# Side jobs queued behind VectorE's weight splits, in smaller portions, in the pass of u of a hybrid block with product-key experts

## The chip, the cores and the metric

The kernel runs on one core of a Trainium2 chip, as one launch. The metric is the time of one execution in microseconds, here the median of several runs. A core has a matrix engine (TensorE, PE in the profile; its weight loads are PEld), VectorE (DVE), ScalarE (ACT), GpSimd (POOL) and SyncE (SP), which mostly issues DMAs. Each engine works through its own instructions in order.

## The reference

One layer over 512 tokens of 1024 features, in float32: a norm, a mixer of differential attention and a gated linear recurrence, an output projection, and then a layer of 16384 experts that are picked per token. The last part is what the change touches, and it is this:

```python
q = (xt @ w_q).reshape(T, 8, 2, 128)
s = einsum('thcd,hcnd->thcn', q, sub_keys)          # 128 keys a side
s1, i1 = top_k(s[:, :, 0], 16)
s2, i2 = top_k(s[:, :, 1], 16)
cand = s1[..., :, None] + s2[..., None, :]          # 256 sums per head
cand_idx = i1[..., :, None] * 128 + i2[..., None, :]
top_s, top_pos = top_k(cand, 16)
expert_idx = take_along_axis(cand_idx, top_pos)
gate = softmax(top_s)
# per token: 8 heads x 16 experts = 128 of 16384
hidden = einsum('td,tkd->tk', xb, u[idx])
act = gelu(hidden) * g
out = einsum('tk,tkd->td', act, v[idx])
```

## The kernel before

The 512 tokens are four blocks of 128. For the last three blocks (384 tokens) the expert layer is computed densely: all 16384 rows of u are multiplied with the tokens in a first pass, the result goes through Gelu, is multiplied with a matrix G that holds each token's gates at its 128 experts and zero elsewhere, and a second pass multiplies with all rows of v. The first block is computed as the reference writes it, with gathers of 128 rows of u per step.

The pass of u is the loop `for c in range(P)` at L718, one chunk of 128 experts each. `dense_u(c)` (L525) loads 512 KB of u (`wu`, a DMA that SyncE issues), splits them into a rounded high part `hi` (ScalarE, L160) and the remainder `lo` (L164), and runs 24 matmuls: 8 pieces of the feature axis, each with hi x hi, hi x lo and lo x hi (L534). The remainder is VectorE's for every third chunk (c = 0, 3, 6, ...) and GpSimd's for the two others (`U_SPLIT`). There are four buffers each of `wu`, `hi` and `lo`, and two PSUM banks of H. ScalarE empties a bank by a Gelu (`gl`, L539) and stores the result to memory (`a_d`); the last 43 chunks stay on chip.

Beside this, the loop hands out two generators' work before each chunk. `jobs` is the chain of routing block 1, building its G, and the same for blocks 2 and 3. `route(b)` is the two levels of top-16 on VectorE (L347 to L351; `sc`, `v`, `i` are the 128-key level and `cand`, `tv`, `ti` the level of 50 candidates a head), the one-hot look-up of indices (`oh` L389 and `ef` L391 on VectorE, `ov` L390 on GpSimd), and the gates: a subtraction on VectorE (L394), `Exp` on ScalarE (L395), sum and division. `build_gates(b)` turns the indices into numbers (`f`, L417), transposes them on TensorE (`tpg`, L420 and L421), compares them with a ramp (`A` L444, `B` L448), scales by the gates (`Bg` L451), multiplies on TensorE (`gq` L456), and stores G (`g_d`). `ug` is `gather_u(0)`: GpSimd issues a gather of 128 rows (`gt`, L469, three buffers), and VectorE forms the dot with the tokens (L472) one step later. After the last dot ScalarE takes one Gelu of them (`hid`, L474).

Each `yield` names a weight; `more(gen, budget)` (L703) steps a generator until the weights reach the budget, `JOBS` = 2.6 and `DOTS` = 2.4 a chunk. What a step takes beyond the budget is not counted later. This sets the order in which the program is traced. A scheduler then lists the instructions of each engine by a simulated time; what is traced under `tc.high_priority()`, as the split is, goes ahead of the rest that is ready.

Block 0's routing runs before the loop, on the same names; its last parts overlap the loop's first chunks.

Of the kernel before, what the change touches and what calls it, by code (L numbers as in the profile page):

```python
# [3 lines left out]

# [7 lines left out]
F32 = mybir.dt.float32  # L12
# [10 lines left out]
P = 128  # L23
# [13 lines left out]
TD = ND * P  # L37
TB = 32
GG = 4
JOBS = 2.6  # L40
DOTS = 2.4
U_SPLIT = ('av', 'ap', 'ap')
V_SPLIT = ("av", "av", "av")
GS = 4096.0
# [9 lines left out]
def block_kernel(ctx: ExitStack, tc: tile.TileContext, a: dict, out: bass.AP):  # L54
# [89 lines left out]
    def mix_t(o, mixedT, i, gain):  # L144
# [6 lines left out]
        nc.scalar.activation(hi, tp, AF.Copy, scale=gain)  # L151
        nc.vector.scalar_tensor_tensor(lo, tp, gain, hi.bitcast(F32), op0=ALU.mult, op1=ALU.subtract)

    def split(src, how="av"):

        hi = wts.tile([P, D], F32R, name="hi", tag="hi", bufs=WS)
        lo = wts.tile([P, D], F32R, name="lo", tag="lo", bufs=WS)
        s = src.rearrange("p k c -> p (k c)") if len(src.shape) == 3 else src
        if how[0] == "a":
            nc.scalar.activation(hi, s, AF.Copy)  # L160
        else:
            nc.vector.tensor_copy(hi, s)
        eng = nc.gpsimd if how[1] == "p" else nc.vector
        eng.tensor_tensor(out=lo, in0=s, in1=hi.bitcast(F32), op=ALU.subtract)  # L164
        return hi, lo

    last = [None]
# [187 lines left out]
    def route(b):  # L355
        v16 = mid.tile([P, 16, 16], F32, name="v16", tag="v16", bufs=EARLY)
        i16 = mid.tile([P, 16, 16], U32, name="i16", tag="i16", bufs=EARLY)
        for r in range(16):
            if r % 2 == 0:
                sc = mid.tile([P, 2, P], F32, name=f"sc{b}", tag="sc", bufs=3)  # L360
                nc.sync.dma_start(sc, sc_d[b, r // 2])
            top16(v16[:, r, :], i16[:, r, :], sc[:, r % 2, :], P)
            yield 1.0
        i16f = mid.tile([P, 8, 2, 16], F32, name="i16f", tag="i16f", bufs=1)
        nc.vector.tensor_copy(i16f.rearrange("p h c k -> p (h c) k"), i16)
        vv = v16.rearrange("p (h c) k -> p h c k", c=2)
        nc.vector.tensor_scalar_mul(i16f[:, :, 0, :], i16f[:, :, 0, :], float(P))
        cand = mid.tile([P, 8, NCAND], F32, name="cand", tag="cand", bufs=1)
        cidx = mid.tile([P, 8, NCAND], F32, name="cidx", tag="cidx", bufs=1)
        for dst, s1, s2 in ((cand, vv[:, :, 0, :], vv[:, :, 1, :]), (cidx, i16f[:, :, 0, :], i16f[:, :, 1, :])):  # L370
            o = 0
            for i, w in enumerate(CAND_W):
                nc.vector.tensor_tensor(out=dst[:, :, o:o + w], in0=s2[:, :, 0:w], in1=s1[:, :, i:i + 1].to_broadcast([P, 8, w]),  # L373
                                        op=ALU.add)
                o += w
            nc.vector.tensor_tensor(out=dst[:, :, o:o + 8], in0=s1[:, :, 8:16], in1=s2[:, :, 0:1].to_broadcast([P, 8, 8]),
                                    op=ALU.add)
        tv = mid.tile([P, 8, 16], F32, name="tv", tag="tv", bufs=1)
        ti = mid.tile([P, 8, 16], U32, name="ti", tag="ti", bufs=1)
        for r in range(8):  # L380
            top16(tv[:, r, :], ti[:, r, :], cand[:, r, :], NCAND)
            yield 0.7
        tif = mid.tile([P, 8, 16], BF16, name="tif", tag="tif", bufs=1)
        nc.vector.tensor_copy(tif, ti)
        ef = mid.tile([P, 8, 16], F32, name="ef", tag="ef", bufs=1)
        for r in range(8):
            oh = mid.tile([P, NCAND, 16], BF16, name="oh", tag="oh", bufs=1)
            ov = mid.tile([P, 16, NCAND], F32, name="ov", tag="ov", bufs=1)
            nc.vector.tensor_tensor(out=oh, in0=iota_c, in1=tif[:, r, None, :].to_broadcast([P, NCAND, 16]), op=ALU.is_equal)  # L389
            nc.gpsimd.tensor_tensor(out=ov.rearrange("p k c -> p c k"), in0=oh, in1=cidx[:, r, :, None].to_broadcast([P, NCAND, 16]), op=ALU.mult)  # L390
            nc.vector.tensor_reduce(ef[:, r, :], ov, axis=AX.X, op=ALU.add)  # L391
            yield 1.4
        g = mid.tile([P, 8, 16], F32, name=f"gate{b}", tag="gate" if b else "gate0")
        nc.vector.tensor_tensor(out=g, in0=tv, in1=tv[:, :, 0:1].to_broadcast([P, 8, 16]), op=ALU.subtract)  # L394
        nc.scalar.activation(g, g, AF.Exp)  # L395
        gs = mid.tile([P, 8], F32, name="gs", tag="gs", bufs=1)
        nc.vector.tensor_reduce(gs, g, axis=AX.X, op=ALU.add)
        nc.vector.reciprocal(gs, gs)
        nc.vector.tensor_tensor(out=g, in0=g, in1=gs[:, :, None].to_broadcast([P, 8, 16]), op=ALU.mult)
        gates[b] = g  # L400
        if b:
            sel[b] = (ef, g)
            return
        ei = mid.tile([P, P], I32, name="ei")
        nc.vector.tensor_copy(ei, ef.rearrange("p h k -> p (h k)"))
        eidx[b] = ei

    def build_gates(b):
# [7 lines left out]
        nc.vector.tensor_single_scalar(i12[:, 1, :], ei, P - 1, op=ALU.bitwise_and)  # L416
        nc.vector.tensor_copy(f12, i12)  # L417
        tp = psu.tile([P, 4, P], F32, name="tpg", tag="tp")
        for i in range(2):
            nc.tensor.transpose(tp[:, i, :], f12[:, i, :], ident)  # L420
        nc.tensor.transpose(tp[:, 2, :], g.rearrange("p h k -> p (h k)"), ident)  # L421
        sT = bld.tile([P, 2, P], F16, name=f"sT{b}", tag="sT", bufs=1)
        nc.vector.tensor_copy(sT, tp[:, 0:2, :])
        gT = bld.tile([P, P], F32, name=f"gT{b}", tag="gT", bufs=1)
# [100 lines left out]
    def dense_u(c):  # L525
        w = wts.tile([P, KC, P], F32, name="wu", tag="w")
        u_load[0] = nc.sync.dma_start(w, a["uT"][c])
        with tc.high_priority():
            hi, lo = split(w, U_SPLIT[c % 3])
        H_ps = psu.tile([P, 512], F32, name="H", tag="H", bufs=2)[:, :TD]  # L530
        for k in range(KC):
            ks = slice(k * P, (k + 1) * P)
            for i, (x, y) in enumerate(((hi, X[0]), (hi, X[1]), (lo, X[0]))):
                nc.tensor.matmul(H_ps, x[:, ks], y[:, k, P:], start=k + i == 0, stop=k == KC - 1 and i == 2)  # L534
        if c >= P - sum(KEEP):
            gl = kept_gl[c] = next(slots)
        else:
            gl = den.tile([P, TD], F32, name="gl", tag="gl", bufs=3)
        nc.scalar.activation(gl, H_ps, AF.Gelu)  # L539
        if c not in kept_gl:  # L540
            nc.scalar.dma_start(a_d[c], gl)

# [157 lines left out]
    vgen = gather_v(0)  # L700
    vp = None

    def more(gen, budget):  # L703
        while budget > 0:
            x = next(gen, None)
            if x is None:
                return False
            budget -= x
        return True

    for c in range(P):
        if vp is None and not more(jobs, JOBS):
            bldx.close()
            vp = ctx.enter_context(tc.tile_pool(name="vp", bufs=2, side="right", reuse_waits="tile"))
            load_g(order[0])
            kept[False] = ctx.enter_context(tc.tile_pool(name="keep2", bufs=1, side="right", reuse_waits="tile"))
        if not more(ug, DOTS) and c < V0_UNTIL:
            next(vgen, None)  # L718
        dense_u(c)
    assert vp is not None  # L720
    psu_x.close()
# [97 lines left out]
```

## Time and profile before

| | us |
|---|---|
| median of 3 runs | 1653.03 (1651.81 to 1653.68) |
| the profiled execution | 1650.1 |
| its span | 1648.3 |
| TensorE busy | 1565.3 (95%) |
| VectorE busy | 1164.1 (71%) |
| ScalarE busy | 633.7 (38%) |
| GpSimd busy | 732.3 (44%) |

The span runs from the first instruction to the last. The profiled execution's own time is 1.8 us longer than its span and 2.9 us under the median. The pass of u starts at 431.32 us and the pass of v at 1102.76; what lies before is the mixer and the scores of the routing. Busy time is an average over stages with different limits, so it is read by stretch. A wait is put down to the instruction that came last.

### The profile page before, as it was taken

The page shows a single profiled execution, that of the slowest core. Times are in us where ns is not written, and L with a number is a line of the kernel's source. Part 1 is how long each engine was busy: PE and PEld are TensorE (multiplying, and loading weights), DVE is VectorE, ACT ScalarE, POOL GpSimd, SP SyncE. Part 2 cuts the span into 40 slices and gives each one's busy share as a digit, 9 for nine tenths or more (in the row PEclk, how much of TensorE's full clock was granted, in tenths as well). Part 3 has the DMA queues.
Part 4 walks back from the last instruction along what each step waited for, and adds up shares of the span by engine and source line. Part 5 has one row for each costly group of instructions (what it writes and reads, how often), then busy time and mean ns, then how long its engine had stood idle before and what let it go on. Part 6 is the DMA issues. An engine that isn't in the chain of part 4 may idle for free.

```text
span 1648.3 us, 22390 instructions
## 1 busy us (share of the span) xinstructions
PE 1565.3 (95%) x8045; PEld 1367.9 (83%) x8045; DVE 1164.1 (71%) x2268; ACT 633.7 (38%) x979; POOL 732.3 (44%) x457
## 2 busy tenths in 40 slices
PE   7999987799989889998999999999999999999998
PEld 5788755588989889898999999998888888888886
DVE  5065553535799899987677665458988888888874
ACT  4475444323333233433443443333333333333332
POOL 3533311433356977775655566643332323323300
PEclk9999988899999989998999999999999999999999
DMA  4421201434546867787888879899999999999982
GB/s 170 156 94 65 77 26 61 156 127 160 172 160 205 300 221 273 250 324 280 292 291 317 286 290 319 300 321 338 381 351 330 335 333 325 340 348 322 342 281 103
DMA packets 173900, 404.70 MB, mean 246 GB/s; under 512 B 14523, under 2 KB 95675, under 8 KB 172252
## 3 DMA queue, kind: packets, MB, share of 16 engines
q1 hardware_dynamic: 124684, 252.31, 44.3%
q0 software_dynamic: 36864, 134.23, 23.0%
q10 hardware_dynamic: 12240, 16.72, 2.8%
q8 instruction: 63, 1.03, 0.2%
q14 instruction: 49, 0.40, 0.1%
HBM read 351.63 MB, written 51.58 MB: 245 GB/s over the span
## 4 chain that ended last, share of the span: by engine, by line
PE 55%; DVE 15%; DMA 2%; POOL 1%; issue 1%; ACT 0%; POOLq 0%; DVEq 0%; ACTq 0%
PE y L576 32%; PE H L534 19%; PE gq L456 4%; DVE gt L472 2%; DVE lo L164 2%; DVE Bg L451 1%; DMA gt<-in_u,ei 1%; DVE ef L391 1%; DVE oh L389 1%; DVE B L448 1%; DVE A L444 1%; DVE cand L373 1%; POOL ov L390 0%; POOL lo L164 0%; DVE sc L349 0%
## 5 line engine op out<-in xcount | busy, mean ns | idle before, releaser
L534 PE MATMUL H<-Xh,hi 128*128 128x384 f32 x1024 | 348.8, 341 | 9.2 <-ACT gl L539 7.9
L534 PE MATMUL H<-Xh,lo 128*128 128x384 f32 x1024 | 348.6, 340 | 3.2 <-DVE lo L164 2.2
L534 PE MATMUL H<-Xl,hi 128*128 128x384 f32 x1024 | 349.5, 341 | 0.0
L482 POOL DMA_INDIRECT gv<-in_v,ei x128 | 154.1, 1204 | 336.2 <-DVE tail L486 303.6
L160 ACT ACTIVATE hi<-wu 128x1024 fp32r<-128x1024 f32 x128 | 135.8, 1061 | 329.2 <-PE H L534 243.8
L164 POOL TENSOR_TENSOR lo<-wu,hi 128x1024 fp32r<-128x1024 f32 x85 | 213.2, 2508 | 105.5 <-ACT hi L160 104.7
L576 PE MATMUL y<-lo,ah 128*128 128x512 f32 x768 | 241.8, 395 | 0.0
L576 PE MATMUL y<-hi,ah 128*128 128x512 f32 x768 | 241.8, 396 | 0.0
L576 PE MATMUL y<-hi,al 128*128 128x512 f32 x768 | 241.8, 395 | 0.0
L534 PEld LDWEIGHTS H<-Xh,hi 128*128 128x128 f32 x1024 | 195.2, 191 | 10.8 <-ACT gl L539 9.2
L469 POOL DMA_INDIRECT gt<-in_u,ei x128 | 158.3, 1237 | 102.4 <-DVE hid L472 71.2
L534 PEld LDWEIGHTS H<-Xh,lo 128*128 128x128 f32 x1024 | 195.2, 191 | 4.5 <-DVE lo L164 3.0
L534 PEld LDWEIGHTS H<-Xl,hi 128*128 128x128 f32 x1024 | 195.5, 191 | 0.0
L567 ACT ACTIVATE ah<-act 128x384 fp32r<-128x384 f32 x128 | 67.1, 525 | 332.0 <-issue 278.1
L472 DVE CUSTOM_DVE_ANT_0 gt<-gt,hn2p 128x1024 f32<-128x1024 f32 x128 | 153.3, 1212 | 52.7 <-DMA gt<-in_u,ei 52.6
L576 PEld LDWEIGHTS y<-hi,ah 128*128 128x128 f32 x768 | 144.4, 188 | 34.9 <-ACT gkFalse L539 0.2
L576 PEld LDWEIGHTS y<-hi,al 128*128 128x128 f32 x768 | 144.4, 188 | 34.8
L576 PEld LDWEIGHTS y<-lo,ah 128*128 128x128 f32 x768 | 144.4, 188 | 34.7
L486 DVE SCALAR_TENSOR_TENSOR tail<-gv,hid,tail 128x1024 f32<-128x1024 f32 x127 | 162.7, 1281 | 11.0 <-DMA gv<-in_v,ei 10.3
L164 DVE TENSOR_TENSOR lo<-wv,hi 128x1024 fp32r<-128x1024 f32 x128 | 156.2, 1220 | 10.3 <-ACT hi L160 10.1
L160 ACT ACTIVATE hi<-wv 128x1024 fp32r<-128x1024 f32 x128 | 134.4, 1050 | 13.9 <-DMA wv<-in_v 7.3
L568 DVE TENSOR_TENSOR al<-act,ah 128x384 fp32r<-128x384 f32 x128 | 73.7, 576 | 72.6 <-ACT ah L567 69.4
(258 smaller groups left out, 2389.6 us busy)
## 6 DMA issues: line engine op xcount, KB each, us to landing
wu<-in_uT SPq DMA_DIRECT2D x128, 512.0 KB
wv<-in_v SPq DMA_DIRECT2D x128, 512.0 KB
g_d<-gs SPq DMA_DIRECT2D x12, 2048.0 KB
G<-g_d SPq DMA_DIRECT2D x32, 768.0 KB
a_d<-gl ACTq DMA_DIRECT2D x85, 192.0 KB
gr<-a_d SPq DMA_DIRECT2D x85, 192.0 KB
w_in<-in_w_in SPq DMA_DIRECT2D x28, 512.0 KB
w_q<-in_w_q SPq DMA_DIRECT2D x16, 512.0 KB
```

The source lines that it names most:

```text
L160: nc.scalar.activation(hi, s, AF.Copy)
L164: eng.tensor_tensor(out=lo, in0=s, in1=hi.bitcast(F32), op=ALU.subtract)
L373: nc.vector.tensor_tensor(out=dst[:, :, o:o + w], in0=s2[:, :, 0:w], in1=s1[:, :, i:i + 1].to_broadcast([P, 8, w]), op=ALU.add)
L456: nc.tensor.matmul(gq[:, t, :], A[:, (t4 + t) // 2, :, t % 2], Bg[:, i, t4 // 4, :, t], start=i == 0, stop=i == 1)
L469: nc.gpsimd.indirect_dma_start(out=t, out_offset=None, in_=a["u"], in_offset=bass.IndirectOffsetOnAxis(ap=ei[:, k:k + 1], axis=0))
L472: nc.vector.tensor_tensor_reduce(out=t, in0=t, in1=hn2p, scale=1.0, scalar=0.0, op0=ALU.mult, op1=ALU.add, accum_out=hid[:, k:k + 1])
L482: nc.gpsimd.indirect_dma_start(out=t, out_offset=None, in_=a["v"], in_offset=bass.IndirectOffsetOnAxis(ap=eidx[b][:, k:k + 1], axis=0))
L486: nc.vector.scalar_tensor_tensor(acc, t, w, acc, op0=ALU.mult, op1=ALU.add)
L534: nc.tensor.matmul(H_ps, x[:, ks], y[:, k, P:], start=k + i == 0, stop=k == KC - 1 and i == 2)
L567: nc.scalar.activation(ah, act, AF.Copy)
L568: nc.vector.tensor_sub(al, act, ah.bitcast(F32))
L576: nc.tensor.matmul(y[b][j], x[:, cs], z[:, j * 512:(j + 1) * 512], start=c == order[0] and i == 0, stop=c == order[-1] and i == 2)
```

## The change

`split` notes VectorE's latest split of a chunk in a table `at`, and `dense_u` notes TensorE's last H matmul and ScalarE's Gelu. `behind(engine)` opens `tc.issue_after(at[engine])`: what is traced in it is ordered behind the noted instruction where it runs on the same engine, and no data passes between them. All steps of `jobs` and `ug` are traced behind VectorE's latest split, the Exp of routing behind ScalarE's latest Gelu, and the transposes behind TensorE's latest H. Both get a `yield 1.5` ahead of them. The table is emptied before the loop. The budgets become 1.7 and 1.25, and what a step takes beyond its budget is taken off the next chunk's. A branch that `V0_UNTIL` = 0 had switched off is gone.

```diff
-JOBS = 2.6
-DOTS = 2.4
+JOBS = 1.7
+DOTS = 1.25
...
+    at = {}
+
+    def behind(engine):
+        return tc.issue_after(at[engine]) if engine in at else nullcontext()
...
-        eng.tensor_tensor(out=lo, in0=s, in1=hi.bitcast(F32), op=ALU.subtract)
+        i = eng.tensor_tensor(out=lo, in0=s, in1=hi.bitcast(F32), op=ALU.subtract)
+        if how[1] != "p":
+            at["DVE"] = i.ins
...
-        nc.scalar.activation(g, g, AF.Exp)
+        yield 1.5
+        with behind("ACT"):
+            nc.scalar.activation(g, g, AF.Exp)
...
-        for i in range(2):
-            nc.tensor.transpose(tp[:, i, :], f12[:, i, :], ident)
-        nc.tensor.transpose(tp[:, 2, :], g.rearrange("p h k -> p (h k)"), ident)
+        yield 1.5
+        with behind("PE"):
+            for i in range(2):
+                nc.tensor.transpose(tp[:, i, :], f12[:, i, :], ident)
+            nc.tensor.transpose(tp[:, 2, :], g.rearrange("p h k -> p (h k)"), ident)
...
-                nc.tensor.matmul(H_ps, x[:, ks], y[:, k, P:], start=k + i == 0, stop=k == KC - 1 and i == 2)
+                mm = nc.tensor.matmul(H_ps, x[:, ks], y[:, k, P:], start=k + i == 0, stop=k == KC - 1 and i == 2)
+        at["PE"] = mm.ins
...
-        nc.scalar.activation(gl, H_ps, AF.Gelu)
+        at["ACT"] = nc.scalar.activation(gl, H_ps, AF.Gelu).ins
...
+    credit = {}
+
     def more(gen, budget):
-        while budget > 0:
+
+        left = credit.get(gen, 0.0) + budget
+        while left > 0:
             x = next(gen, None)
             if x is None:
                 return False
-            budget -= x
+            left -= x
+        credit[gen] = left
         return True
 
+    at.clear()
     for c in range(P):
-        if vp is None and not more(jobs, JOBS):
+        with behind("DVE"):
+            busy = more(jobs, JOBS)
+        if vp is None and not busy:
...
-        if not more(ug, DOTS) and c < V0_UNTIL:
-            next(vgen, None)
+        with behind("DVE"):
+            more(ug, DOTS)
         dense_u(c)
```

The lines that the profile calls L394, L395, L417, L420 and L451 are L402, L405, L427, L432 and L463 in the changed file. In the lists below the names are those of the section on the kernel; a number behind a name tells apart tiles of one name.

VectorE ahead of the first block's gate subtraction (`gate_3543`, for which ScalarE's first Exp waits), from behind the split of chunk 6, before:

```order
L349 MATCH_REPLACE cand<-tv,cand 128x50 x8
L348 MAX_INDEX i_5931<-v_5930,sc_5932 128x8 x2
L348 MAX_INDEX i_5931<-v_5930,sc_5944 128x8 x2
L347 MAX v_5930<-sc_5996 128x8
L365 CAST i16f<-i_2582 128x256
L350 MAX tv<-cand 128x8 x8
L349 MATCH_REPLACE sc_5932<-v_5930,sc_5932 128x128 x2
L349 MATCH_REPLACE sc_5944<-v_5930,sc_5944 128x128 x2
L348 MAX_INDEX i_5931<-v_5930,sc_5996 128x8
L367 TENSOR_SCALAR i16f<-i16f 128x8x16
L351 MAX_INDEX ti<-tv,cand 128x8 x8
L394 TENSOR_TENSOR gate_3543<-tv 128x128
```

and now:

```order
L357 MATCH_REPLACE cand<-tv,cand 128x50 x8
L373 CAST i16f<-i_2582 128x256
L358 MAX tv<-cand 128x8 x8
L375 TENSOR_SCALAR i16f<-i16f 128x8x16
L359 MAX_INDEX ti<-tv,cand 128x8 x8
L402 TENSOR_TENSOR gate_3543<-tv 128x128
```

The searches, the replacements and the maximum of the 128-key level (the rows with `sc_`), which belong to a later block, no longer stand there; the six rows of block 0 are the same.

VectorE around the conversion of block 1's indices (`f`, which TensorE's first transposes read; `sT` is the transposes' result on its way back), before; the split shown is chunk 33's:

```order
L472 ISA gt,hid_3619<-gt,hn2p 128x1024
L472 ISA hid_3619 128x1
L415 TENSOR_SCALAR i_3930<-ej_3929 128x128
L416 TENSOR_SCALAR i_3930<-ej_3929 128x128
L367 TENSOR_SCALAR i16f<-i16f 128x8x16
L417 CAST f_3931<-i_3930 128x256
L472 ISA gt,hid_3619<-gt,hn2p 128x1024
L472 ISA hid_3619 128x1
L391 TENSOR_REDUCE ef<-ov 128x16
L389 TENSOR_TENSOR oh<-iota_c,tif 128x800
L164 TENSOR_TENSOR lo<-wu,hi 128x1024
L423 CAST sT_3940<-tpg 128x256
```

and now; the split at the end is chunk 30's:

```order
L484 ISA gt,hid_3614<-gt,hn2p 128x1024
L484 ISA hid_3614 128x1
L427 CAST f_4064<-i_4063 128x256
L484 ISA gt,hid_3614<-gt,hn2p 128x1024
L484 ISA hid_3614 128x1
L484 ISA gt,hid_3614<-gt,hn2p 128x1024
L484 ISA hid_3614 128x1
L435 CAST sT_4110<-tpg 128x256
L437 TENSOR_SCALAR gT_4112<-tpg 128x128
L456 TENSOR_TENSOR A<-iota_n,sT_4110 128x2048
L460 TENSOR_TENSOR B<-iota_n,sT_4110 128x2048
L170 TENSOR_TENSOR lo<-wu,hi 128x1024
```

Before, the conversion stands behind chunk 30's split, with chunk 33's split five rows after it and the copy `sT` behind that; now it stands behind chunk 27's split (not shown), and the copy and the first A and B stand ahead of chunk 30's. A dot and its second row (`hid`, which reads out the sum) stand between. `oh` and `ef` of the next block are no longer among these rows.

## Rows read from the trace of the kernel before

**Rows 1.** The page: the kernel's span.
```profile
span 1648.3 us, 22390 instructions
```

**Rows 2.** By stretch: us, engines' busy us, TensorE's clock, DMA share, GB/s.
```profile
431.00:751.00 320.00, 285.40 (x1680) 277.53 (x1679) 306.11 (x810) 116.29 (x164) 219.84 (x118) 0.95 0.70 241
751.00:1102.00 351.00, 349.69 (x2173) 344.16 (x2173) 219.55 (x260) 136.72 (x206) 210.36 (x128) 1.00 0.86 303
```

**Rows 3.** The chain by time: start us, us, what.
```profile
770.08 1.88 PE gq L456 x16
771.95 13.52 PE H L534 x78
1102.76 534.61 PE y L576 x2291
```

**Rows 4.** Timeline of TensorE, first H: start us, us, operation.
```profile
431.32 0.42 PE L534 MATMUL H<-Xh,hi 128*128 128x384 f32 x1
```

**Rows 5.** Waits of TensorE, 431 to 751 us: total us, times, longest.
```profile
PE tpg L420 <- DVE f L417: 15.1, 2, 7.7
PE gq L456 <- DVE Bg L451: 8.4, 5, 2.5
PE H L534 <- ACT gl L539: 7.9, 3, 6.9
PE H L534 <- DVE lo L164: 2.2, 1, 2.2
```

**Rows 6.** By stretch, after two long waits of TensorE.
```profile
468.00:475.00 7.00, 7.00 (x32) 7.00 (x33) 7.00 (x30) 2.73 (x4) 5.16 (x3) 0.78 0.55 183
751.00:765.00 14.00, 14.00 (x91) 13.37 (x91) 10.94 (x13) 6.07 (x10) 10.22 (x6) 0.88 0.70 225
```

**Rows 7.** Timeline, splits of u's chunks on VectorE (DVE) and GpSimd (POOL).
```profile
432.77 1.20 DVE L164 TENSOR_TENSOR lo<-wu,hi 128x1024 fp32r<-128x1024 f32 x1
619.61 3.57 DVE L164 TENSOR_TENSOR lo<-wu,hi 128x1024 fp32r<-128x1024 f32 x1
619.67 2.41 POOL L164 TENSOR_TENSOR lo<-wu,hi 128x1024 fp32r<-128x1024 f32 x1
748.99 1.21 DVE L164 TENSOR_TENSOR lo<-wu,hi 128x1024 fp32r<-128x1024 f32 x1
```

**Rows 8.** The chain by time, two stretches.
```profile
459.38 1.05 DVE i L348 x4
463.15 1.45 DVE ti L351 x8
...
727.17 14.62 DMA gt<-in_u,ei
```

**Rows 9.** VectorE, 431 to 751: xcount, busy us, mean ns, idle before.
```profile
L472 DVE CUSTOM_DVE_ANT_0 gt<-gt,hn2p 128x1024 f32<-128x1024 f32 x46 | 55.1, 1207 | 11.3 <-DMA gt<-in_u,ei 11.3
L164 DVE TENSOR_TENSOR lo<-wu,hi 128x1024 fp32r<-128x1024 f32 x20 | 33.6, 1682 | 0.0
L391 DVE TENSOR_REDUCE ef<-ov 128x16 f32<-128x800 f32 x32 | 31.1, 973 | 1.6 <-POOL ov L390 1.6
L389 DVE TENSOR_TENSOR oh<-iota_c,tif 128x800 bf16<-128x800 bf16 x32 | 28.5, 890 | 0.0
L451 DVE TENSOR_TENSOR Bg<-B,gp 128x2048 f16<-128x2048 f16 x20 | 27.2, 1390 | 0.0
L444 DVE TENSOR_TENSOR A<-iota_n,sT 128x2048 f16<-128x2048 f16 x10 | 17.8, 1778 | 0.0
```

**Rows 10.** Timeline of ScalarE around the first Exp.
```profile
454.11 1.28 ACT L395 ACT_TABLE_LOAD   x1 [0.39 <-ACT gl L539]
464.82 0.31 ACT L395 ACTIVATE gate<-gate 128x128 f32<-128x128 f32 x1 [9.43 <-DVE gate L394]
467.38 0.49 ACT L539 ACTIVATE gl<-H 128x384 f32<-128x384 f32 x1
```

**Rows 11.** Groups on VectorE, 751 to 1102: the dots.
```profile
L472 DVE CUSTOM_DVE_ANT_0 gt<-gt,hn2p 128x1024 f32<-128x1024 f32 x83 | 99.4, 1215 | 41.4 <-DMA gt<-in_u,ei 41.3
```

More of the change, by code (lines that the diff above doesn't have):

```diff
@@ L1 @@
 import math
-from contextlib import ExitStack
+from contextlib import ExitStack, nullcontext
 from functools import partial
```

## The prediction

> **What bounds the kernel now.** I read the page's span first, then the windows by stage, then what TensorE waits for, then the chain, then VectorE's groups. The span is 1648.3 us [rows 1]. In the stage in which u is multiplied (431 to 1102.76 us, where the chain takes up the y matmuls and stays with TensorE for the last 534.61 us [rows 3]) two halves differ: until 751 us TensorE is busy 285.40 of 320 us and VectorE 306.11, that is 96%; after it TensorE is busy 349.69 of 351 and VectorE 219.55 [rows 2]. So VectorE paces the first half and TensorE the second. The v pass is TensorE's own and nothing of the change reaches it.
>
> TensorE's own work in the pass: the chain has 78 H matmuls in 13.52 us, 0.1733 each, so 4.16 us for a chunk's 24, and 1.88 us for 16 gq [rows 3]. 128 chunks make 532.4, the 48 gq blocks 90.0, the transposes some 1.6: 624 us. The pass lasts from the first H at 431.32 [rows 4] to 1102.76, 671.4, so 47 us are lost. By cause, in the first half [rows 5]: transposes tpg behind the conversion f 15.1 (2 times), gq behind Bg 8.4 (5 times), H behind the Gelu that empties its bank 7.9 (one wait is 6.9), H behind VectorE's split 2.2: 33.6 in all. The rest is small gaps and half clock: in the 7 us after the long wait before 468 TensorE was busy throughout at a granted 0.78, and in the 14 us after the wait before 751 at 0.88 [rows 6]; the levels are 1.2 and 2.4 GHz, so these cost 7 x 0.22 = 1.5 and 14 x 0.12 = 1.7 us.
>
> The same from VectorE's side: its split for chunk 3 starts at 432.77, the one for chunk 60 at 748.99 [rows 7]: 316.2 us for 57 chunks. TensorE needs for 57 chunks with the 20 gq blocks of that stretch 57 x 4.16 + 20 x 1.88 = 274.7, so about 41.5 of the 47 us arise here.
>
> **The change part by part.**
>
> *Less VectorE work before chunk 60.* Smaller amounts (1.7 and 1.25 for 2.6 and 2.4), with the overshoot now charged to the next chunk, spread the jobs over more chunks. Counted over VectorE's new order from the split of chunk 3 to that of chunk 60, against the old: 149 fewer small routing instructions (409 to 260), 8 fewer oh and ef (32 to 24), 6 more dots (45 to 51), 2 more A and B each, 4 more Bg. Small ones: four index searches took 1.05 and eight of the 50-wide kind 1.45 [rows 8], so 0.18 to 0.26 each: 27 to 39, taken at 33. ef and oh are 0.97 and 0.89: 14.9 less. Dots 1.21, A 1.78 (B taken alike), Bg 1.39 [rows 9]: 7.3 + 7.1 + 5.6 = 20 more. Net 28 us less (22 to 34). VectorE's stretch shrinks from 316 to about 288, its gather waits of 11.3 [rows 9] included. TensorE now needs 57 x 4.16 + 24 x 1.88 = 282 there. The two engines come out nearly even: VectorE stops being the pace by a hair, not by a margin.
>
> *What was taken out of there* (the third block's top-16, two dozen Bg, the rest of the dots) lands behind chunk 60, where VectorE has 351 - 220 = 131 us free [rows 2]. I cost it at nothing. If that cover fails, every VectorE microsecond beyond it would show on TensorE at full price; the count for chunks 60 to 126 goes from some 212 to 250 us against 66 x 4.16 + 24 x 1.88 = 320, so it does not.
>
> *Transposes.* In the old order the first conversion f stands behind the split of chunk 30, yet TensorE takes its transposes at chunk 30.2, a stretch in which VectorE was far behind; now f stands behind the split of chunk 27 and TensorE takes them at chunk 26.8. f comes three dots, an ef and the splits' own 1.2 later, some 6 us or 1.4 chunks; VectorE's rows from chunk 3 to 30 add up to 109 us against 27 x 4.16 + 8 (the Exp's stall) = 120 on TensorE, so it is the full lead of its four buffers ahead by then and both long waits (7.7 and 7.4) [rows 5] go. What is late next is gq: the first Bg now ends VectorE's stretch after chunk 30, the first gq waits at chunk 30.2. A Bg with its inputs is up to four instructions behind: 1.4 (one Bg) to 5.6 (four). I take 2.5, the longest Bg wait of before. The second transposes 1 (0 to 2), later gq 3 (0 to 5, for five waits of 8.4 before).
>
> *First Exp.* It waits on ScalarE from 455.4 to 464.82 for VectorE's first subtraction, with a Gelu queued behind it until 467.38 [rows 10]; TensorE stalls 6.9 us there. Routing 0 is not put behind anything, and in the new order the Exp stands behind four Gelus instead of five: one chunk, 4.16, sooner. Before the subtraction stand ten 128-wide searches, maxima and replacements fewer, and some 3 more of them ahead of the split: 13 x 0.26 = 3.4 sooner at most, 2.6 at least. The wait becomes 6.9 + 4.16 - 3.0 = 8.1 (7.7 to 8.5): this stall stays, slightly dearer. Exps 2 to 4 move to 10, 43 and 84 Gelus deep and cost nothing on TensorE as long as VectorE is there in time.
>
> *Edges.* issue_after adds only an order on one engine; no instruction is added. The added waits are instructions queued behind jobs on VectorE: while a job's dot waits for its gather, the next split waits too, and TensorE behind it once its four buffers are through.
>
> *DMAs.* SP's loads of the third routing's scores now stand between the wu of chunks 70 and 76, and one waits for VectorE's top-16 of the buffer: 0 to 3, taken 1.5. g_d stores and the first G load keep several chunks of margin: 0. The wait near 1094 for the last dot stays: 1.5.
>
> *Half clock.* One long stall remains for three: 4 (2 to 6), from the 1.5 and 1.7 above and a little for each short one.
>
> Sum of losses after: 8.1 + 2.5 + 1 + 3 + 1.5 + 1.5 + 4 + 2 (small gaps) = 23.6 against 47: 23.5 us less. Span 1624.8, and with the 1.8 us around the span, 1626.6 for an execution like the profiled one at 1650.1. The median of before was 1653.0, 2.9 above it, so I predict 1630 us. With the small gaps at 1 to 3, the low ends add up to 13.6 of loss (1620), the high ends to 34.6 (1641).
>
> **A rule weighed.** A split on VectorE that ran beside GpSimd's split (3.57 from 619.61; GpSimd's 2.41 from 619.67) took three times the 1.20 of an undisturbed one [rows 7]; over 20 splits the mean was 1.682 [rows 9], an excess of 0.48 x 20 = 9.6 us. The Trainium skill, "SBUF — State Buffer" (The single rule), says that a VectorE instruction with two SBUF inputs and a GpSimd instruction that reads SBUF exclude each other for the whole instruction. The pair at 619.6 agrees. By the rule at its full, taken as the worst case, two GpSimd splits of 2.4 in each of the 19 stretches from chunk 3 to 60 would hold VectorE 91 us, the even balance above would be lost, and the sum would come out above 1700. By the rows the splits lose a tenth of that, the same pairs stood side by side before, and the measured durations of the other groups hold their share already: 1630. I go by the rows and give the rule no chance beyond its part in (a).
>
> **The rivals.**
>
> (a) *VectorE still paces chunks 30 to 54.* The balance is 282 to 288, so 6 us of excess, and another 6 to 10 of gather or GpSimd blocking, pass on to TensorE. For it: VectorE at 96% [rows 2] and a gather seen 14.62 us under way [rows 8]. Against it: four buffers of lead. Losses 23.6 + 12 to 16, 36 to 40: median about 1643 (1641 to 1649).
>
> (b) *Nearly every wait goes.* VectorE keeps ahead from chunk 20 and only the Exp and the end remain: loss about 13, median about 1619. Against it: the even balance.
>
> (c) *It does not do what it says.* The waits move: Exp plus 1.2, transposes replaced by gq waits of the same size, loss 44 to 50: median 1650 to 1656.
>
> (d) *Slower: dots in front of the splits.* Every dot now stands in VectorE's queue between splits, spread evenly, and waits there for its landing. Place: chunks 18 to 60. The wait per dot is 11.3 / 46 = 0.25 us before 751 and 41.4 / 83 = 0.50 after [rows 9, 11]. At 0.50 the 51 dots add 12.7 us (that is case a); it decides from 0.25 + 23.5 / 51 = 0.71 us per dot. At 1.0, where gathers run beside 512 KB loads and the a_d stores, 38 us more: median about 1668; at 0.9, 1663. Against it: three gather buffers are issued ahead, and a slower VectorE gives them time.
>
> **How the numbers follow.** Forecast 0.52, (a) 0.18, (b) 0.08, (c) 0.07, (d) 0.15. A measurement of this kernel tells about 0.2%, 3.3 us, from no change. Faster: 0.52 + 0.18 + 0.08 = 0.78; the same: 0.07; slower: 0.15. The forecast's own range is 1620 to 1642 with what runs differ by. The range that holds 8 of 10 takes in (a) and half of (c) above, and the most of (b) below: 1617 to 1654.
>
> **What would show it.** Right: in the profile after, TensorE's wait for f is gone or under 2 us, its wait at the first Gelu after the Exp is 7.5 to 8.5 at about 463 us, the y matmuls begin near 1079, VectorE's splits are 12.5 to 17 us apart through chunk 60, and the first half's VectorE share falls under 93%. Wrong: H waiting on VectorE's split in several places (a, d), Bg waits above 8 us together (c), gather waits on VectorE of more than 36 us before chunk 60 (d), or a pass that still lasts over 665 us.

## The result

The changed kernel takes 1631.31 us (median of 4 runs, 1629.26 to 1632.68) against 1652.42 for the kernel before: a ratio of 0.9873, 95% interval 0.9856 to 0.9891. Run again beside three experiments it was 0.9911 (0.9879 to 0.9943) of before. The prediction was 1630 us, 1626.6 for the profiled execution; that one took 1629.26, with a span of 1627.5.

The chain and TensorE's timeline of the changed kernel (start us, us, what) bound the pass of u, beside [rows 3, 4]:

```profile
431.44 0.42 PE L546 MATMUL H<-Xh,hi 128*128 128x384 f32 x1
...
1081.91 534.62 PE y L589 x2291
```

It runs from 431.44 to 1081.91: 650.5 us against 671.4. The v pass behind it lasts 534.62, before 534.61. With the same 624 us of own work TensorE loses 26.5 us and not 47.4. The busy time by stretch in the changed kernel, beside [rows 2], and then in three shorter stretches (columns as there):

```profile
431.00:751.00 320.00, 303.24 (x1854) 296.72 (x1853) 283.81 (x606) 125.79 (x180) 218.91 (x121) 0.98 0.76 268
751.00:1082.00 331.00, 327.52 (x2006) 322.98 (x2005) 247.36 (x465) 128.35 (x190) 213.60 (x125) 0.99 0.84 296
431.00:560.00 129.00, 115.03 (x651) 113.25 (x649) 112.41 (x335) 46.31 (x61) 89.86 (x50) 0.97 0.65 219
560.00:640.00 80.00, 77.21 (x484) 75.12 (x485) 78.44 (x167) 29.48 (x44) 57.67 (x33) 0.97 0.85 296
640.00:760.00 120.00, 120.00 (x778) 117.19 (x777) 101.96 (x134) 52.88 (x79) 77.00 (x44) 1.00 0.84 311
```

and the three of the kernel before:

```profile
431.00:560.00 129.00, 119.19 (x676) 117.59 (x675) 122.10 (x534) 47.64 (x63) 79.33 (x43) 0.97 0.60 202
560.00:640.00 80.00, 65.72 (x372) 63.48 (x372) 77.20 (x156) 26.36 (x37) 63.53 (x37) 0.89 0.74 247
640.00:760.00 120.00, 109.49 (x694) 104.99 (x693) 114.12 (x131) 46.63 (x71) 83.21 (x44) 0.94 0.78 281
```

Up to 560 us TensorE is busy less than before (115.03 for 119.19). From 560 to 640 it gains 11.5 us and from 640 to 760 another 10.5, with the clock at 1.00 in the last: the gain lies between about chunk 27 and chunk 60, and VectorE has 12 us less to do from 640 to 760. At the end of that stretch it is VectorE that waits. Between 706 and 748 us it stands idle for ScalarE's `hi` and for TensorE's gq; before the change it had neither wait ahead of 751 (VectorE's waits, 431 to 751):

```profile
DVE lo L170 <- ACT hi L166: 8.6, 3, 4.5
DVE A L456 <- PE gq L468: 7.9, 3, 3.9
```

What TensorE still waits for in the whole pass (total us, times, longest), beside [rows 5]:

```profile
PE tpg L432 <- DVE f L427: 9.3, 2, 7.1
PE H L546 <- ACT gl L552: 6.2, 1, 6.2
PE H L546 <- POOL lo L170: 2.8, 3, 1.3
PE gq L468 <- DVE Bg L463: 1.9, 2, 1.3
```

These are 20.2 us; the rest of the 26.5, some 6, is half clock and small gaps. One of the two long transposes' waits is still there, now at 562 us. The wait behind the first Exp is 6.2 us, a little shorter than before, on ScalarE:

```profile
459.77 0.31 ACT L405 ACTIVATE gate<-gate 128x128 f32<-128x128 f32 x1 [8.47 <-DVE gate L402]
462.34 0.49 ACT L552 ACTIVATE gl<-H 128x384 f32<-128x384 f32 x1
```

The Exp comes 5.05 us sooner than in [rows 10].

How far TensorE has come, read from the timeline: the start of each chunk's first H behind that of chunk 0, in us, and at last the first y matmul. The kernels are those of the next section.

| kernel | chunk 18 | 30 | 48 | 60 | first y |
|---|---|---|---|---|---|
| before | 84.2 | 138.8 | 255.3 | 332.4 | 671.3 |
| changed | 83.0 | 145.7 | 247.6 | 314.8 | 650.3 |
| changed, again | 83.7 | 146.4 | 248.2 | 319.9 | 655.4 |
| amounts alone | 84.2 | 139.2 | 255.8 | 329.7 | 674.3 |
| orderings alone | 85.3 | 150.8 | 260.6 | 329.3 | 668.6 |
| without VectorE's ordering | 84.2 | 138.6 | 252.7 | 324.7 | 660.5 |
| VectorE's ordering alone | 85.2 | 146.6 | 247.9 | 319.1 | 654.3 |
| late Exp | 82.4 | 143.6 | 246.1 | 321.7 | 657.2 |
| splits to VectorE | 83.7 | 143.2 | 261.6 | 328.5 | 660.6 |
| dots from 36 | 84.2 | 149.8 | 260.0 | 326.8 | 687.0 |
| late Exp and dots from 36 | 82.9 | 146.5 | 244.5 | 312.7 | 673.4 |
| dots' amount 2.4 | 83.7 | 146.3 | 256.2 | 334.2 | 671.0 |
| transposes held | 83.8 | 138.5 | 247.8 | 316.2 | 675.9 |
| transposes held, late Exp | 80.9 | 136.0 | 245.1 | 314.7 | 671.2 |

Each row is one execution. Two executions of the changed kernel differ by 0.7 us at chunks 30 and 48 and by 5.1 at chunk 60 and at the first y.

A chunk's place does not tell all of TensorE's work, since gq blocks stand between the chunks, and not the same number in each kernel: ahead of chunk 48 there are 10 before and 14 now. With TensorE's own work taken off (4.16 us a chunk and 1.88 a gq block, as in the prediction), this is what it has lost by the start of a chunk, in us:

| kernel | chunk 30 | 48 | 60 |
|---|---|---|---|
| before | 14.0 | 36.8 | 47.1 |
| changed | 20.9 | 21.6 | 21.9 |
| changed, again | 21.6 | 22.2 | 27.0 |
| orderings alone | 25.7 | 34.6 | 34.6 |
| late Exp | 18.8 | 20.1 | 28.9 |
| splits to VectorE | 16.5 | 31.8 | 31.9 |
| dots from 36 | 17.5 | 28.3 | 28.3 |
| late Exp and dots from 36 | 14.2 | 14.5 | 16.1 |
| dots' amount 2.4 | 21.5 | 30.2 | 41.4 |
| transposes held | 13.7 | 23.6 | 32.7 |
| transposes held, late Exp | 11.2 | 21.0 | 34.8 |

### The profile page after: what moved, and what is told of

The parts are those of the page before. It is cut to its first block, busy times and chain, and to the rows that moved or that the text cites. A ratio compares the mean times of both kernels' runs of the same rounds, so it can differ in the third digit from the quotient of the medians.

```text
span 1627.5 us, 22379 instructions
## 1 busy us (share of the span) xinstructions
PE 1560.2 (96%) x8045; PEld 1363.0 (84%) x8045; DVE 1169.7 (72%) x2268; ACT 634.1 (39%) x979; POOL 733.9 (45%) x457
## 4 chain that ended last, share of the span: by engine, by line
PE 82%; DVE 9%; DMA 3%; POOL 3%; issue 2%; ACT 1%; SPq 0%; POOLq 0%; DVEq 0%; ACTq 0%
PE y L589 33%; PE H L546 22%; PE acct L212 7%; PE acc L197 5%; PE gq L468 5%; PE accq L197 5%; POOL ov L398 1%; DVE gt L484 1%; DMA gt<-in_u,ei 1%; PE sp L349 1%; POOL lo L170 1%; DVE oh L397 1%; PE hsc L266 1%; PE lg L311 1%; DMA wu<-in_uT 1%
## 5 line engine op out<-in xcount | busy, mean ns | idle before, releaser
L481 POOL DMA_INDIRECT gt<-in_u,ei x128 | 164.8, 1288 | 82.1 <-DVE hid L484 48.5
L484 DVE CUSTOM_DVE_ANT_0 gt<-gt,hn2p 128x1024 f32<-128x1024 f32 x128 | 153.6, 1210 | 47.6 <-DMA gt<-in_u,ei 47.4
L589 PEld LDWEIGHTS y<-hi,ah 128*128 128x128 f32 x768 | 143.6, 187 | 35.6 <-ACT gkFalse L552 0.2
L589 PEld LDWEIGHTS y<-lo,ah 128*128 128x128 f32 x768 | 143.6, 187 | 35.6
L589 PEld LDWEIGHTS y<-hi,al 128*128 128x128 f32 x768 | 143.6, 187 | 35.6
L170 DVE TENSOR_TENSOR lo<-wv,hi 128x1024 fp32r<-128x1024 f32 x128 | 156.0, 1219 | 18.8 <-ACT hi L166 18.2
L166 ACT ACTIVATE hi<-wv 128x1024 fp32r<-128x1024 f32 x128 | 134.3, 1049 | 12.5 <-issue 5.5
```

The source lines that it names most:

```text
L170: i = eng.tensor_tensor(out=lo, in0=s, in1=hi.bitcast(F32), op=ALU.subtract)
L481: nc.gpsimd.indirect_dma_start(out=t, out_offset=None, in_=a["u"], in_offset=bass.IndirectOffsetOnAxis(ap=ei[:, k:k + 1], axis=0))
L484: nc.vector.tensor_tensor_reduce(out=t, in0=t, in1=hn2p, scale=1.0, scalar=0.0, op0=ALU.mult, op1=ALU.add, accum_out=hid[:, k:k + 1])
L589: nc.tensor.matmul(y[b][j], x[:, cs], z[:, j * 512:(j + 1) * 512], start=c == order[0] and i == 0, stop=c == order[-1] and i == 2)
```

## The experiments

All are edits of the changed kernel. Ratios are to the kernel before on the same chip. The changed kernel itself ran beside the last three edits alone; the others are compared with it by their ratios.

**Amounts alone.** The three orderings are off:

```diff
-        return tc.issue_after(at[engine]) if engine in at else nullcontext()
+        return nullcontext()
```

> The smaller amounts and the carried overshoot alone, with none of the three orderings (the two new steps of 1.5 stay). Theory A, the prediction's: the smaller amounts thin VectorE's work before chunk 60 and bring the gain; then 1632 to 1640 us. Theory B: the amounts act only through the orderings, since without them the scheduler takes a job up as soon as its inputs are there, whenever it was traced; then the waits of before come back (both transposes near 7.5 us, five Bg waits) and the time is 1649 to 1656. The order of this kernel's instructions (transposes at chunks 30.2, 46 and 58, as before the change) speaks for B.

1.0024 (1.0009 to 1.0039). The waits of before are back, and the Gelu of the last dot holds ScalarE longer at the end:

```profile
PE tpg L432 <- DVE f L427: 12.6, 2, 7.7
PE gq L468 <- DVE Bg L463: 8.5, 5, 2.5
...
PE H L546 <- ACT gkFalse L552: 4.6, 1, 4.6
```

Theory B: without an ordering the amounts gain nothing.

**Orderings alone.** The old amounts, and what is over is dropped:

```diff
-JOBS = 1.7
-DOTS = 1.25
+JOBS = 2.6
+DOTS = 2.4
...
-        credit[gen] = left
+        credit[gen] = 0.0
```

> All orderings, with the old amounts 2.6 and 2.4 and no carrying over. VectorE's order from the split of chunk 3 to that of chunk 60 holds 405 small instructions, 25 oh, 46 dots and 24 Bg: by the durations of before 296 us, as much as in the kernel before (298) and 30 more than in the changed one. Theory A (what counts is how much VectorE has before chunk 60): TensorE loses 35 to 47 us again, 1641 to 1653. Theory B (what counts is that splits come ahead of jobs): 1629 to 1638, with H waiting on splits under 3 us.

0.9999 (0.9984 to 1.0013), by theory A. Orderings without smaller amounts gain nothing either; the first transposes wait 6.6 us, and the Gelu of the last dots holds ScalarE and TensorE for 7.7:

```profile
PE H L546 <- ACT gkFalse L552: 7.7, 1, 7.7
PE tpg L432 <- DVE f L427: 7.0, 2, 6.6
```

**Without VectorE's ordering.**

```diff
-        return tc.issue_after(at[engine]) if engine in at else nullcontext()
+        return tc.issue_after(at[engine]) if engine in at and engine != 'DVE' else nullcontext()
```

> The changed kernel without the ordering behind VectorE's splits; the orderings of Exp and of the transposes and the new amounts stay. VectorE's order up to chunk 60 is the old one but for three instructions; the third transposes move from chunk 58 to 85. Both theories say that the first transposes' wait comes back (7 to 8 us). If the late third transposes alone are worth their old wait, 7.4 us and the 1.7 of half clock behind it, the time is 1641 to 1646; if that wait only moves to VectorE's next late product, 1648 to 1655.

0.9959 (0.9942 to 0.9976), 1642.34 us, in the first range: the later third transposes, with the later Exps, are worth 6.1 us against before (1648.45 on this chip) and 10.8 against the amounts alone (1653.13), and the first wait is 7.7 as before.

**VectorE's ordering alone.** The same line with `engine == 'DVE'`.

> The changed kernel with the ordering behind VectorE's splits alone: Exp and transposes are free to be placed. VectorE's order is that of the changed kernel; the second Exp stands 7 Gelus deep and not 10, the third 36 and not 43, the fourth 78 and not 84; the transposes stay at chunks 26.8, 48.6 and 85.4. If VectorE's ordering is the whole of the gain, 1629 to 1634 us. If the ordering of Exp is worth something, the second Exp waits on ScalarE for a subtraction that is not ready, TensorE stalls another 4 to 8 us near chunk 8, and the time is 1635 to 1641.

0.9899 (0.9877 to 0.9921), 1632.98 us: between the two readings of the whole change (0.9873 and 0.9911), so with the new amounts VectorE's ordering is the whole of the gain, within what runs differ by. Behind the second Exp TensorE did stall, but for 1.22 us at 478 and not 4 to 8.

**Late Exp.** Block 0's Exp and normalising move into a generator of their own behind `build_gates(1)`; the line that places it:

```diff
-    jobs = chain(routes[1], build_gates(1), routes[2], build_gates(2), routes[3], build_gates(3))
+    jobs = chain(routes[1], build_gates(1), normalise(0), routes[2], build_gates(2), routes[3], build_gates(3))
```

> The changed kernel with the Exp and the normalising of block 0's gates, which are needed only after the last dot, moved behind the gates of block 1 (32 Gelus deep); nothing is left out. Theory A (the stall of 6.4 us at the first Exp and the 1.6 of half clock behind it are a loss of their own): 1621 to 1626 us. Theory B (TensorE, not held there, only reaches the next late product of VectorE sooner: the first transposes wait some 14 us and not 7): 1629 to 1634.

0.9913 (0.9879 to 0.9946), 1636.0 us: no gain, and above both ranges. The stall at the Exp is gone and TensorE is 8 us ahead at chunk 9 (37.6 for 45.6), but at chunk 18 only 0.6 (82.4 for 83.0). There it waited for GpSimd's split (TensorE's timeline):

```profile
508.84 0.69 PE L551 MATMUL H<-Xh,lo 128*128 128x384 f32 x1 [4.83 <-POOL lo L170]
```

f started 128.1 us behind the first H, in the changed kernel 130.4: TensorE was 8 us ahead at chunk 9, VectorE 2.4 at f. This is theory B in kind, by another wait than the one it named: the first transposes waited 7.1 us again and not 14, and a second wait of theirs came on top (6.7 us at 694).

**Splits to VectorE.**

```diff
-            hi, lo = split(w, U_SPLIT[c % 3])
+            hi, lo = split(w, 'av' if c in (19, 22, 25, 28) else U_SPLIT[c % 3])
```

> The changed kernel with the splits of chunks 19, 22, 25 and 28 on VectorE and not on GpSimd: 4.9 us more for VectorE, 9.6 less for GpSimd, in the stretch ahead of the wait of 7.1 us for f. Theory P (f is late because VectorE is blocked by GpSimd's instructions and waits for its products there): f's wait falls under 3.5 us and H's waits for GpSimd's splits (2.8) under 1.5; 1623 to 1629. Theory V (f is late because VectorE has too much of its own): f's wait grows to 9 to 12 us; 1632 to 1638.

0.996 (0.9943 to 0.9976), 1642.76 us: neither. f came 12.3 us sooner (118.1 us behind the first H), and H no longer waited for GpSimd's splits, as theory P has it, but the scheduler had moved the transposes up with f, to chunk 25.0, and they waited 5.6 and 6.1 us (two waits, 11.7 together); chunk 48 began at 261.6.

**Dots from chunk 36.**

```diff
-            more(ug, DOTS)
+            if c >= 36:
+                more(ug, 1.75)
```

> The changed kernel with dots handed out only from chunk 36 on, at 1.75 a chunk. Up to chunk 30 no gather is issued by GpSimd and VectorE has 17 dots fewer; after chunk 60 VectorE has 21 more. Theory P (GpSimd's gathers, products and splits together delay VectorE there): VectorE's waits for ov and the long oh go, the first transposes, now at chunk 23.7, wait under 2 us, and unless the last dots come late the time is 1620 to 1626. If the wait of the last dot at the end of the pass takes it back: 4 to 8 us there, 1627 to 1632. If transposes wait as before, P falls.

1.0103 (1.0064 to 1.0141), 1666.74 us: a miss on both sides. f came 17.2 us sooner (113.2 us behind the first H), but the transposes stood at chunk 23.7 and waited 5.5, and VectorE's waits for `ov` grew (25.4 us for 10.0 up to 570): theory P falls by its own condition. At the end of the pass:

```profile
1118.17 0.79 PE L589 MATMUL y<-hi,ah 128*128 128x512 f32 x1 [29.31 <-DVE hid L484]
```

29.3 us and not 4 to 8: at 1.75 a chunk the dots were not made up for.

**Late Exp and dots from 36.** Both edits.

> Both of the two edits, the late Exp of block 0 and dots from chunk 36 on. If the stall at the first Exp and the wait for f are separate losses, TensorE loses under 12 us in the pass and the time is 1612 to 1619. If VectorE sets the pace up to chunk 30 whatever stalls TensorE there, the gain over the kernel with late dots alone is under 3 us.

1.0048 (1.003 to 1.0065), 1656.42 us, with 28.8 us for the last dot: a miss on both sides. It is 10.3 us faster than with late dots alone, where the second theory had under 3, and TensorE loses 49.4 us in the pass, where the first had under 12. At chunk 48 it was the earliest of all, 244.5, and up to chunk 60 it had lost the least, 16.1.

**Dots' amount 2.4.**

```diff
-DOTS = 1.25
+DOTS = 2.4
```

> The changed kernel with the dots' amount back at 2.4; the jobs' 1.7, the carrying over and the orderings stay. VectorE's order has the same counts in every stretch as the changed kernel's. Theory A (only the jobs' amount matters, the dots being held by their gathers): 1628 to 1634 us. Theory B (more dots at once hold splits back): 1635 to 1642, with VectorE's waits for gathers before 751 us above 9.

0.9975 (0.9961 to 0.9989), 1644.17 us, theory B and more. Up to chunk 30 VectorE's order is the same; behind it the dots stand in other places. What VectorE waits for there, 431 to 751 us, here and in the changed kernel:

```profile
DVE gt L484 <- DMA gt<-in_u,ei: 19.6, 7, 5.8
```

```profile
DVE gt L484 <- DMA gt<-in_u,ei: 6.7, 6, 3.0
```

19.6 us for 6.7. A gather was 13.02 us under way from 695.10, two dots waited 4.11 and 5.78 us for their landings, and the Bg behind them came 8.2 us late for TensorE (its waits for Bg in the pass):

```profile
PE gq L468 <- DVE Bg L463: 19.6, 7, 8.2
```

The profiled execution, 1651.74 us, is the slowest of the ten, so its waits overstate the median's loss.

**Transposes held.**

```diff
-JOBS = 1.7
+JOBS = 2.2
...
-        yield 1.5
+        yield 48.0 if b == 1 else 1.5
         with behind("PE"):
```

> The changed kernel with the step ahead of block 1's transposes weighing 48 and not 1.5, and the jobs' amount 2.2 and not 1.7, which makes room for it: TensorE takes these transposes at chunk 30.0 and not 26.8, f stands where it stood. Theory A (the wait of 7.1 us for f is there because the transposes stand three chunks too early on TensorE): that wait goes, the second and third shrink or stay, 1621 to 1626 us. Theory B (VectorE and GpSimd pace TensorE up to chunk 30 anyway): H waits for splits or gq for Bg instead, the same 6 to 8 us, 1628 to 1635.

1.0024 (1.0005 to 1.0044), 1654.49 us. The first transposes no longer wait and chunk 30 begins at 138.5, 7.2 us sooner; at chunk 48 nothing is left of it (247.8 for 247.6): gq waits 7.8 us for the first Bg, which is theory B's mechanism; the time is far above both ranges. The jobs' amount changed with it, so the two are not told apart. What makes it slower comes later: the second transposes 6.0, and 9.6 near the end, where the Gelu of the dots stands earlier on ScalarE:

```profile
PE gq L468 <- DVE Bg L463: 10.9, 2, 7.8
PE H L546 <- ACT gkFalse L552: 10.7, 2, 9.6
```

**Transposes held, late Exp.** Both edits.

> The same with the Exp of block 0 moved behind the gates of block 1 as well. Under theory A both losses go and TensorE loses under 14 us in the pass: 1614 to 1620. Under theory B chunk 30 still begins some 140 to 146 us behind the first chunk, as in every kernel so far, and the time is that of the kernel with the held transposes, within 4 us.

0.9994 (0.9976 to 1.0011), 1648.37 us. Chunk 30 begins at 136.0, outside theory B's 140 to 146, and chunk 48 at 245.1, 2.5 us sooner than in the changed kernel with both stalls gone: theory B holds at chunk 48, not at 30. The time is 6.1 us under that of the held transposes, where theory B had 4 at most.

**The changed kernel again.**

> The changed kernel itself, beside the three others on one chip: 0.985 to 0.990 of before. In its profile the wait for f near 562 us and the one at the first Gelu are again there, each within 0.5 us of 7.1 and 6.2.

0.9911 (0.9879 to 0.9943), a little above the 0.985 to 0.990 expected. Both waits are there (7.1 and 6.2); a second one of 3.1 us at 684 for f, which the first profile did not have, shows how little VectorE is ahead there.

No version was faster than the changed kernel clear of what its two readings differ by. Not tried: the old jobs' amount with the dots' new one, and carrying over by itself.

## Why the prediction was right, and where it was not

**The bound and the place of the gain: right.** Of the 47.4 us that TensorE lost before, 47.1 lie ahead of chunk 60, the part that VectorE paces; the rest had nothing to give back. Within that part the whole gain lies between chunks 30 and 60: the changed kernel loses 1.0 us there (5.4 in the repeat) where 33.1 were lost. Up to chunk 30 it loses 7 more (20.9 for 14.0), because the first transposes, whose wait is nearly the same (7.1 for 7.7), now stand ahead of that chunk and no longer behind it; that wait set aside, nothing changed there and some 25 us between 30 and 60 became 1. At the end of that part VectorE is no longer the pace: it waits for TensorE's side, 16.5 us in all. The v pass did not move.

**The sum: right by terms that cancel, which is luck.** In us of TensorE's loss, in the one profiled execution (the last row but one is what is left over; in the repeat the sum is 31.4):

| term | predicted | measured |
|---|---|---|
| first Exp | 8.1 | 6.2 |
| first transposes | 0 | 7.1 |
| second and third transposes | 1 | 2.2 |
| gq for Bg | 5.5 | 1.9 |
| H for GpSimd's splits | in the small gaps | 2.8 |
| SP's loads | 1.5 | 0 |
| last dot | 1.5 | 0 |
| half clock and small gaps | 6 | 6.3 |
| sum | 23.6 | 26.5 |

*Transposes* is the step that failed: "both long waits go". The wait of the third block's transposes went (2.2 us are left of 7.4); that of the first block's stayed (7.1 for 7.7). The step set VectorE's own rows from chunk 3 to 30, 109 us, against TensorE's 120 and found VectorE four buffers ahead. VectorE reached chunk 30's split at 567.8 us, 135 behind chunk 3's. This is the stretch between the two (columns as in [rows 2]) and what VectorE waited for in it:

```profile
432.38:567.79 135.41, 119.22 (x666) 117.45 (x665) 118.33 (x338) 47.12 (x62) 95.36 (x53) 0.95 0.66 220
DVE ef L399 <- POOL ov L398: 10.0, 6, 1.9
DVE gt L484 <- DMA gt<-in_u,ei: 5.6, 4, 3.0
```

VectorE is busy 118.3 us and waits 17 (1.3 of them for scores). So of the 26 us that the step had too few, 17 are waits, which it put at nothing, and 9 are rows that took longer than it priced them. Between the same splits before, the waits for ov were 1.6 us and those for gathers 7.1. There VectorE had 530 instructions and now 338, so less stands between an oh and its ef; that this is why it now waits for ov no run shows. Of the rows, the 16 oh took 1.40 us on the mean for the 0.89 of [rows 9], 8.2 us in all, and one cast 2.5 us too long; the splits were near their price. The groups on VectorE from 495 to 570 us (count, busy us, mean ns, idle before), where the most of this lies; the three first rows are the changed kernel's, the two last those of before:

```profile
L397 DVE TENSOR_TENSOR oh<-iota_c,tif 128x800 bf16<-128x800 bf16 x9 | 15.9, 1770 | 0.0
L170 DVE TENSOR_TENSOR lo<-wu,hi 128x1024 fp32r<-128x1024 f32 x5 | 10.6, 2119 | 0.0
L399 DVE TENSOR_REDUCE ef<-ov 128x16 f32<-128x800 f32 x10 | 9.8, 980 | 6.5 <-POOL ov L398 6.5
...
L389 DVE TENSOR_TENSOR oh<-iota_c,tif 128x800 bf16<-128x800 bf16 x12 | 10.7, 889 | 0.0
L164 DVE TENSOR_TENSOR lo<-wu,hi 128x1024 fp32r<-128x1024 f32 x6 | 8.5, 1424 | 0.0
```

An oh took 0.56 undisturbed (at 501.68) and 1.77 on the mean here, a split 2.12 for 1.20. In the timeline the long oh lie beside GpSimd's splits and end 0.44 us behind them; the long splits lie beside GpSimd's products ov and end 0.94 to 0.96 behind those. Over the whole pass of the changed kernel an oh beside no split or product of GpSimd took 0.55 to 0.58 us (15 of them), one beside took 1.75 to 3.27 (14). An oh, and the cast `ej` ahead of f:

```profile
543.05 3.27 DVE L397 TENSOR_TENSOR oh<-iota_c,tif 128x800 bf16<-128x800 bf16 x1
543.45 2.43 POOL L170 TENSOR_TENSOR lo<-wu,hi 128x1024 fp32r<-128x1024 f32 x1
...
557.68 2.74 DVE L424 CAST ej<-ef 128x128 int32<-128x128 f32 x1
557.98 2.35 POOL L170 TENSOR_TENSOR lo<-wu,hi 128x1024 fp32r<-128x1024 f32 x1
...
561.88 0.28 DVE L427 CAST f<-i 128x256 f32<-128x256 int32 x1
562.22 0.48 PE L432 MATMUL tpg<-ident,f 128*128 128x128 f32 x1 [7.15 <-DVE f L427]
```

The cast `ej` took 2.74 us there, the same cast for block 0 (`ei`, at 502.16) 0.21. In both pairs VectorE's row starts first, by 0.40 and 0.30 us, and yet it is the long one; GpSimd's splits keep 2.35 to 2.43 us in this stretch. ef, a reduction, kept its 0.98 beside a GpSimd split too (at 515.13). The dots, whose second input `hn2p` lies in PSUM, kept 1.21 beside GpSimd's splits and products (62 of them). The Trainium skill, "SBUF — State Buffer" (Who interferes with whom), has it so: a cast in a mode that uses both ports contends with GpSimd, an instruction with two inputs in SBUF contends with a GpSimd instruction that reads SBUF, and a reduction on this chip never does. These rows agree, though none of them says in which mode the cast ran. So the rule that the prediction weighed and set at "a tenth" was worth more here: oh, splits and cast took 10.9 + 4.6 + 2.5 = 18 us longer in these 75 than alone, where in the same 75 of the kernel before oh and splits took 3.9 + 1.3 = 5 us longer. That the waits and these rows together made f late is argued from the rows; taking four splits off GpSimd did bring f 12.3 us sooner, and with it the transposes, so that TensorE did not gain.

**The stalls are not separate losses.** The prediction added TensorE's waits as if each could go by itself. The tables of chunks say otherwise. At chunk 48 the late Exp (8 us of stall and half clock taken away) had left 1.5 us of loss less, the held transposes 2.0 more, both together 0.6 less, where two executions of the changed kernel differ by 0.6: VectorE comes to its products when it comes, and TensorE waits for one or for another. It is no law: with dots from 36 the late Exp took 13.8 us off the loss at chunk 48 (14.5 for 28.3), where a wait of 5.9 for the second transposes went as well. TensorE's own work to there is 48 x 4.16 and 10 to 17 gq blocks, 218 to 232; no kernel was under 244.

**The amounts: the count alone did not decide.** The prediction took the gain from 28 us less VectorE work before chunk 60. The count is needed: with the old amounts in the same orderings (296 us of rows) nothing was gained. But with the old dots' amount alone VectorE has the count of the changed kernel, and by the medians on one chip 4.5 us are left of the 14.9 that the changed kernel gains there (in the profiled execution, the slowest, nothing: the pass took 671.0 us, before 671.3). There the dots stand where their gathers have not landed. This is rival (d), "dots in front of the splits", at 19.6 / 51 = 0.38 us of waiting per dot; the changed kernel's is 6.7 / 54 = 0.12, half of before's 0.25 [rows 9]. It told from less than the 0.71 that the rival set; that each landing also holds up the Bg behind it is the likely reason, seen once in the chain at 708 to 717 us. How much of the gain is the jobs' amount with the dots' new one stays open.

**Edges: right in kind.** VectorE's ordering carries the gain: with the new amounts and nothing else it is worth the whole (0.9899), and without it the amounts do little (0.9959 with the two other orderings, 1.0024 with none). *What was taken out* came as priced: after 751 us VectorE is busy 247.36 of 331, 28 more than before, and TensorE 327.52. *Half clock* and the small gaps are known only as what is left over, 6.3 us for 6.

**First Exp:** its size was 1.9 us off: the Exp came 5.05 us sooner, where the step had 3 for the subtraction that it waits for.

**The signs it named.** Two came: the y matmuls begin at 1081.9 (near 1079), and VectorE's share of the first half is 283.81 of 320, 89% (under 93). Three did not: the wait for f is 7.1 us (under 2), the one behind the first Exp 6.2 (7.5 to 8.5), and VectorE's splits are 9.7 to 25.0 us apart up to chunk 60 (12.5 to 17). None of the signs of being wrong came. So the time and the place were right, and the picture of VectorE up to chunk 30 was not.

## What to carry to other kernels

When one engine paces another, a stall of the second is not a loss until it is shown that the first is ahead from there on: follow how far the work has come at a few fixed points, and not only the sum of waits. Portions and orderings gained here only together. The reading, which no run of its own shows, is that an ordering behind a recent instruction binds only if the portion is small enough for the work to be handed out at the pace at which it runs. And a sum of an engine's rows is not its time: add what it waits for between them. Where two engines come out nearly even, a count of work says that a gain is possible, and the places of the few waiting instructions say whether it comes.

## What was not expected of the hardware

A cast of 128 x 128 that takes 0.21 us took 2.74 beside GpSimd's split of 2.35, thirteen times as long. And dots kept back were not made up: with dots from 36 the last 40 came 3.15 us apart on average, with GpSimd waiting for a free buffer and VectorE for landings in turn, and the last came at 1116.9 us, where TensorE had ended its H matmuls at 1088.5.
